# State-space mixer: decays, convolution and product moved off GpSimd; h formed anew with the norm's row; banks emptied by ScalarE

## The chip, the cores and the metric

One core of one Trainium2 chip. The metric is the device time of one execution, in microseconds (us). Names used below: PE is TensorE (PEld its weight loads), DVE is VectorE, ACT is ScalarE, POOL is GpSimd, SP the queue that issues most transfers.

## The reference, cut to what matters

Twelve units follow one another on 256 tokens of width 1024: a first block (two mixers, a feed-forward, a mixture of experts) and a second block. The unit of this case is the state-space mixer of the second block:

```
proj = h @ w_in                                    # h = rmsnorm(x) * gain; 1024 -> 8256
z, xbc, dt_raw = split(proj)
xbc = silu(conv5(xbc, conv_w) + conv_b)            # centred depthwise, 5 taps
xs, b_f, c_f, b_b, c_b = split(xbc)                # 32 heads of 64; 8 groups, state 128
dt = softplus(dt_raw + dt_bias);  cum = cumsum(dt * a)
scores = (c @ b^T) * exp(where(lower, cum_q - cum_k, -inf)) * dt_k
y = scores @ xs  + the same run backwards  + xs * d_skip
y = rmsnorm(y * silu(z)) @ w_out
```

With 256 tokens and chunks of 128 each direction has three 128x128 blocks per head: two on the diagonal, which are masked, and one beside it, which is not.

## The kernel before, in words

The tokens lie along the free axis, the channels on the partitions. Every weight of 128x2048 numbers is loaded by SP into a `wraw` tile (three in flight) and split into a high and a low part, in two halves: ScalarE writes `whi` (L211), VectorE writes `wlo` as the difference (L212). A product is three matmuls (`mm3`, L269): high by high, high by low, low by high. `proj` (L518) takes one weight, makes 2x8x3 = 48 matmuls into a PSUM bank `pj` (three of them) and hands the bank to a function that empties it.

The mixer's method is `ssd` (L1920). Its operands `hh`, `hl` are the split of x times the gain, made while the unit before ends; the norm's factor 1/rms per token (`st["r"]`, a row copied to all partitions at L484) is not in them, and each bank is multiplied by that row when it is emptied. First come the step sizes: `ssd_dt` (L1854) turns a 64x256 bank into dt and its running sum `cum` by some 25 short VectorE instructions, writes `cum` to DRAM as `cumd` (L1881), and transposes three tables of log-factors into `stok`. Then eight groups g of four heads follow; each has four projections:

- `x`, `f`, `b` (`conv`, L1929): VectorE empties the bank into a padded tile `cz*` (L1931), ScalarE makes the first tap with the bias (L1936), and four more taps for two 128-channel halves follow, each a multiply-add of 128x256 on VectorE (`stt`, L287); for the second half of `x` POOL does them, as a product (L1942) and a sum (L1943). ScalarE applies Silu (L1947).
- `z` (`gate`, L1950): VectorE empties the bank times the row into `sz` (L1952), ScalarE applies Silu (L1953).

`ssd_decay` (L1896) makes the decays E of a group, for each direction a tile of 4 heads x 3 blocks x 128 (128x1536): SP reads the rows of `cumd` to all partitions into `crow` (L1903, two transfers, one buffer), POOL subtracts the per-partition table (L1911), adds a mask of -1e30 (L1912) and forms the block beside the diagonal (L1915), five instructions of 128x512 per direction; ScalarE takes the exponential (L1917). It is called at the end of group g; `scan(g)` (L1956) runs in group g+1 behind the `f` projection: transposes of xs to `xd` (L1966), the c-by-b matmuls into a bank, and a VectorE product of E with that bank (L1975, 128x1536). `scan_out(g)` (L1978) comes behind the `z` projection of group g+1: sixteen matmuls of E with xd, the skip term on VectorE (L1989), the product with `sz` on POOL (L1990), ScalarE's high half `yh` (L1994), VectorE's low half `yl` (L1995), and ScalarE's squares that POOL adds up (`sq_add`, L417 to L420). After group 7 the output projection runs as a `Down` (L569), whose matmuls need the four `acc` banks.

Each engine works its instructions off in a fixed order. That order is made when the kernel is built: a scheduler goes by the program's order, in which `first()` (L264) and `high_priority(...)` pull instructions forward, and by its estimate of when inputs are ready.

Of the kernel before, what the change touches and what calls it, by code (L numbers as in the profile page):

```python
# [10 lines left out]
F32 = mybir.dt.float32  # L11
# [8 lines left out]
T = 256  # L20
# [7 lines left out]
NEG = -1e30  # L28

# [217 lines left out]
class Kernel:  # L247
# [1587 lines left out]
    def ssd_consts(self, pool):  # L1835
# [3 lines left out]
        for m, op in zip(S["mask"], (OP.is_lt, OP.is_gt)):  # L1839
            nc.vector.tensor_scalar(m, self.jp, 0.0, NEG, op0=op, op1=OP.mult)  # L1840
# [13 lines left out]
    def ssd_dt(self, pool, b, r):  # L1854
# [31 lines left out]
        for o, c, l in ((0, 0, 127), (32, 1, 128)):  # L1886
            rs, cs = slice(o, o + 32), slice(c * 128, (c + 1) * 128)
            self.stt(off[rs], dt[rs, cs], cum[rs, l:l + 1], cum[rs, cs], OP.add, OP.subtract)
        v.tensor_sub(p, cum, dt)
        b = self.bank("ms")  # L1890
        for i, src in enumerate((p[:, 0:128], p[:, 128:256], off)):
            self.tr(b[:, 64 * i:64 * (i + 1)], src)
# [3 lines left out]
    def ssd_decay(self, pool, g):  # L1896


        nc, S = self.nc, self.S
        cr = pool.tile([128, 2, 4, T], F32, name="crow", bufs=1)  # L1900
        src = S["dram"].rearrange("(r h) t -> r h t", r=2)[:, 4 * g:4 * g + 4, :]
        for r in range(2):
            nc.sync.dma_start(cr[:, r], src[r][None].to_broadcast([128, 4, T]))  # L1903
        out = []
        for r in range(2):
            E = pool.tile([128, 4, 3, 128], F32, name="E", bufs=3)
            hs = slice(4 * g, 4 * g + 4)
            for c in range(2):
                d = E[:, :, 2 * c, :]
                cc = S["tok"][:, c, r, hs][:, :, None].to_broadcast([128, 4, 128])  # L1910
                nc.gpsimd.tensor_sub(d, cr[:, r, :, c * 128:(c + 1) * 128], cc)  # L1911
                nc.gpsimd.tensor_add(d, d, S["mask"][r][:, None, :].to_broadcast([128, 4, 128]))  # L1912
            oc = S["tok"][:, 2, r, hs][:, :, None].to_broadcast([128, 4, 128])
            t = slice(128, 256) if r == 0 else slice(0, 128)
            nc.gpsimd.tensor_add(E[:, :, 1, :], cr[:, r, :, t], oc)  # L1915
            out.append(E)
            nc.scalar.activation(E, E, AF.Exp)  # L1917
        return out

    def ssd(self, pool, tail):  # L1920
# [8 lines left out]
        def conv(n, g, b):  # L1929
            z = S["cz"][n, g % 2 if n == "x" else 0]  # L1930
            v.tensor_mul(z[:, :, 2:T + 2], v2(b), st["r"][:, None, :].to_broadcast([128, 2, T]))  # L1931
# [5 lines left out]
            for k in range(1, 5):  # L1937
                for j in range(2):
                    w = cw[:, 48 * k + tl[j]:48 * k + tl[j] + 1]
                    if n == "x" and j:  # L1940
                        t = pool.tile([128, T], F32, name="cvt", bufs=1)
                        nc.gpsimd.tensor_mul(t, z[:, j, k:k + T], w.to_broadcast([128, T]))  # L1942
# [573 lines left out]
```

## Time and profile before

| | us |
|---|---|
| runs | 2808.49, 2814.82, 2814.09 (median 2814.09) |
| the profiled execution | 2806.44 |
| its span, first to last instruction | 2804.6 |
| PE busy | 2622.2 (93%) |
| DVE busy | 2178.5 (78%) |
| ACT busy | 1582.7 (56%) |
| POOL busy | 564.0 (20%) |

The profiled execution lies 7.65 us under the median of the runs, and 1.8 us of its time lie outside the span. The shares are means over twelve units with different limits, so the mixer is read by its own stretch: the norm's row is ready at 1693 us, the gates of the eight groups are emptied between 1722.7 and 1974.5 us, and the last scan ends at about 1990 us.

### The profile page before, as it was taken

What the parts mean: (1) busy time and instruction counts of PE and PEld (TensorE: products, weight loads), DVE (VectorE), ACT (ScalarE), POOL (GpSimd) and SP (SyncE); (2) the same over time, 40 slices, a digit from 0 to 9 for tenths busy, and PEclk for the clock granted to TensorE, in tenths of its full rate; (3) what the DMA queues carried; (4) which work ended last, traced back from release to release, by engine and by line L of the source; (5) the groups of instructions that cost most, each with busy time, mean ns of one, the idle gap of its engine ahead of it and who ended that gap; (6) DMA issues with size and microseconds to landing.
All of it is one profiled execution on the core that took longest, in us unless ns stands there. A gap on an engine that the chain in (4) does not pass through costs nothing. (4 is left out here: it accounts for less than half of the span.)

```text
span 2804.6 us, 50551 instructions
## 1 busy us (share of the span) xinstructions
PE 2622.2 (93%) x20739; PEld 2446.0 (87%) x20739; DVE 2178.5 (78%) x3100; ACT 1582.7 (56%) x2222; POOL 564.0 (20%) x490
## 2 busy tenths in 40 slices
PE   8999968989999999999998998887899999989999
PEld 6789967789999999999778997777799999979998
DVE  6989986869998999988876568999665675665666
ACT  5343336657777777777663445766444454465444
POOL 2413982310000000000000005776110010240000
PEclk9999988999999999999998999999999999999999
DMA  7476764256999999999763554434445555552553
GB/s 276 167 270 248 279 210 150 91 214 258 349 338 355 339 353 365 342 325 372 250 213 140 197 178 152 151 139 147 151 166 196 186 175 193 195 188 72 182 194 121
DMA packets 109203, 623.07 MB, mean 222 GB/s; under 512 B 10049, under 2 KB 10065, under 8 KB 56353
## 3 DMA queue, kind: packets, MB, share of 16 engines
q1 hardware_dynamic: 107664, 612.05, 61.2%
q0 software_dynamic: 1296, 7.68, 0.7%
q8 instruction: 165, 2.70, 0.4%
q14 instruction: 78, 0.63, 0.1%
HBM read 616.49 MB, written 3.21 MB: 221 GB/s over the span
## 5 line engine op out<-in xcount | busy, mean ns | idle before, releaser
L212 DVE TENSOR_TENSOR wlo<-wraw,whi 128x1024 fp32r<-128x1024 f32 (+1 forms) x1046 | 1284.3, 1265 | 250.1 <-ACT whi L211 247.3
L211 ACT ACTIVATE whi<-wraw 128x1024 fp32r<-128x1024 f32 (+1 forms) x1046 | 1046.5, 1050 | 668.6 <-issue 353.8
L269 PE MATMUL pj<-hh,whi 128*128 128x256 f32 (+1 forms) x2672 | 757.8, 284 | 54.0 <-DVE czb L1931 38.5
L269 PE MATMUL pj<-hh,wlo 128*128 128x256 f32 (+1 forms) x2672 | 754.3, 282 | 4.1 <-DVE wlo L212 4.0
L269 PE MATMUL pj<-hl,whi 128*128 128x256 f32 (+1 forms) x2672 | 754.2, 282 | 1.2 <-DVE hl L287 1.2
L269 PEld LDWEIGHTS pj<-hh,whi 128*128 128x128 f32 (+1 forms) x2672 | 514.9, 193 | 58.9 <-issue 29.3
L269 PEld LDWEIGHTS pj<-hh,wlo 128*128 128x128 f32 (+1 forms) x2672 | 514.4, 193 | 7.9 <-DVE wlo L212 6.8
L269 PEld LDWEIGHTS pj<-hl,whi 128*128 128x128 f32 (+1 forms) x2672 | 514.8, 193 | 3.0 <-DVE hl L287 2.3
L269 PE MATMUL pj<-whi,hg 128*128 128x256 f32 x2112 | 382.2, 279 | 0.0
L269 PEld LDWEIGHTS pj<-whi,hg 128*128 128x128 f32 x2112 | 325.6, 188 | 11.2 <-issue 8.7
L269 PE MATMUL pj<-wlo,hg 128*128 128x256 f32 x1056 | 294.0, 278 | 0.0
L269 PE MATMUL acc<-mh,whi 128*128 128x256 f32 x880 | 245.5, 279 | 13.9 <-ACT whi L211 13.9
L269 PE MATMUL acc<-mh,wlo 128*128 128x256 f32 x880 | 245.8, 279 | 7.0 <-DVE wlo L212 7.0
L269 PE MATMUL acc<-ml,whi 128*128 128x256 f32 x880 | 245.7, 279 | 1.6 <-DVE ml L284 1.6
L269 PEld LDWEIGHTS pj<-wlo,hg 128*128 128x128 f32 x1056 | 198.6, 188 | 3.7 <-issue 2.1
L269 PEld LDWEIGHTS acc<-mh,whi 128*128 128x128 f32 x880 | 167.2, 190 | 14.1 <-ACT whi L211 14.1
L441 POOL TENSOR_TENSOR rc<-var,mhalf 128x2 f32<-128x2 f32 x2 | 1.4, 705 | 878.4 <-DVE var L1803 877.1
L417 POOL TENSOR_TENSOR ss<-sq 128x256 f32<-128x256 f32 x11 | 11.9, 1083 | 825.1 <-ACT sq L410 592.2
L269 PEld LDWEIGHTS acc<-mh,wlo 128*128 128x128 f32 x880 | 167.1, 190 | 8.1 <-DVE wlo L212 8.1
L269 PEld LDWEIGHTS acc<-ml,whi 128*128 128x128 f32 x880 | 167.1, 190 | 2.2 <-DVE ml L284 2.2
L269 PE MATMUL acc<-whi,mml 128*128 128x512 f32 x352 | 139.1, 399 | 0.7 <-DVE mml L284 0.7
L269 PE MATMUL acc<-wlo,mmh 128*128 128x512 f32 x352 | 139.6, 397 | 0.0
(721 smaller groups left out, 4424.6 us busy)
## 6 DMA issues: line engine op xcount, KB each, us to landing
wraw<-in_o_exp_down_dram SPq DMA_DIRECT2D x88, 1024.0 KB, 5.8
wraw<-in_ffn_w_gu_dram SPq DMA_DIRECT2D x88, 1024.0 KB, 5.0
wraw<-in_o_exp_gate_dram SPq DMA_DIRECT2D x87, 1024.0 KB, 5.9
wraw<-in_o_exp_up_dram SPq DMA_DIRECT2D x87, 1024.0 KB, 6.0
wraw<-in_ffn_w_down_dram SPq DMA_DIRECT2D x44, 1024.0 KB, 5.1
wraw<-in_ssd_cols_dram SPq DMA_DIRECT2D x32, 1024.0 KB, 4.9
wraw<-in_e_mod_ffn_w_t_dram SPq DMA_DIRECT2D x12, 1024.0 KB, 5.0
wraw<-in_o_mod_mix_w_t_dram SPq DMA_DIRECT2D x12, 1024.0 KB, 5.0
```

Source lines behind the costliest of these rows:

```text
L211: nc.scalar.activation(hi[:, cs], t[:, cs], AF.Copy)
L212: nc.vector.tensor_sub(lo[:, cs], t[:, cs], f32(hi[:, cs]))
L269: self.nc.tensor.matmul(out, lhsT, rhs, start=start, stop=stop, skip_group_check=True)
L417: nc.gpsimd.tensor_add(ss[0], sq[:, 0, :], sq[:, 1, :])
L441: nc.gpsimd.tensor_tensor(r, v, self.mhalf.to_broadcast([128, n]), op=OP.pow)
```

## The change

- E is loaded directly: SP reads the rows of `cumd` into the E tiles themselves (four transfers per group in place of two, 1.5 times the bytes written; four E buffers instead of three; `crow` is gone). VectorE subtracts the whole table at once (128x1536), clamps the two diagonal blocks from above at 88.722 (128x1024, every third block left out), ScalarE takes the exponential as before. `ssd_decay(g)` is called behind the `x` projection of group g instead of at its end.
- The mask becomes a table of 0 and 1 and moves from the exponent to the c-by-b bank: VectorE writes the two masked blocks (128x256) and ScalarE copies the third (128x128) into a new SBUF tile `scb`; the product with E then has both inputs in SBUF.
- The taps of the second half of `x` become VectorE multiply-adds; the product with `sz` goes to VectorE.
- h is formed anew once the row 1/rms is there: eight VectorE instructions of 128x256 (x times gain times row) and four splits of 128x512 (ScalarE copy, VectorE difference), with raised priority. From then on the banks need no factor: ScalarE empties them (`conv` by a copy, `gate` by Silu straight from the bank). The banks of dt and of the first `x`, which were multiplied before, keep the factor on VectorE.

```diff
--- before.py
+++ after.py
@@ -26,6 +26,8 @@
 MID = 3
 EPS = 1e-6
 NEG = -1e30
+
+LOGMAX = 88.722
 
 SPLIT_ORDER = {"s": -30, "f1_0": -100, "e": -200, "f2_0": 50}
 
@@ -1836,8 +1838,8 @@
         nc = self.nc
         S = self.S = {}
         S["mask"] = [pool.tile([128, 128], F32, name=f"smask{i}") for i in range(2)]
-        for m, op in zip(S["mask"], (OP.is_lt, OP.is_gt)):
-            nc.vector.tensor_scalar(m, self.jp, 0.0, NEG, op0=op, op1=OP.mult)
+        for m, op in zip(S["mask"], (OP.is_ge, OP.is_le)):
+            nc.vector.tensor_scalar(m, self.jp, 0.0, None, op0=op)
         go = S["go"] = pool.tile([64, T], F32, name="sgo")
         nc.gpsimd.memset(go, 1.0)
         nc.gpsimd.memset(go.rearrange("p (c i) -> p c i", i=128)[:, :, 0:1], 0.0)
@@ -1885,10 +1887,10 @@
         off = s2[:, 0:128]
         for o, c, l in ((0, 0, 127), (32, 1, 128)):
             rs, cs = slice(o, o + 32), slice(c * 128, (c + 1) * 128)
-            self.stt(off[rs], dt[rs, cs], cum[rs, l:l + 1], cum[rs, cs], OP.add, OP.subtract)
+            self.stt(off[rs], cum[rs, cs], cum[rs, l:l + 1], dt[rs, cs], OP.subtract, OP.subtract)
         v.tensor_sub(p, cum, dt)
         b = self.bank("ms")
-        for i, src in enumerate((p[:, 0:128], p[:, 128:256], off)):
+        for i, src in enumerate((p[:, 0:128], off, p[:, 128:256])):
             self.tr(b[:, 64 * i:64 * (i + 1)], src)
         tok = S["tok"] = pool.tile([128, 3, 2, 32], F32, name="stok")
         v.tensor_copy(tok, b[:, :192].rearrange("p (i r h) -> p i r h", i=3, r=2))
@@ -1896,28 +1898,23 @@
     def ssd_decay(self, pool, g):
 
 
+
         nc, S = self.nc, self.S
-        cr = pool.tile([128, 2, 4, T], F32, name="crow", bufs=1)
         src = S["dram"].rearrange("(r h) t -> r h t", r=2)[:, 4 * g:4 * g + 4, :]
-        for r in range(2):
-            nc.sync.dma_start(cr[:, r], src[r][None].to_broadcast([128, 4, T]))
         out = []
         for r in range(2):
-            E = pool.tile([128, 4, 3, 128], F32, name="E", bufs=3)
-            hs = slice(4 * g, 4 * g + 4)
-            for c in range(2):
-                d = E[:, :, 2 * c, :]
-                cc = S["tok"][:, c, r, hs][:, :, None].to_broadcast([128, 4, 128])
-                nc.gpsimd.tensor_sub(d, cr[:, r, :, c * 128:(c + 1) * 128], cc)
-                nc.gpsimd.tensor_add(d, d, S["mask"][r][:, None, :].to_broadcast([128, 4, 128]))
-            oc = S["tok"][:, 2, r, hs][:, :, None].to_broadcast([128, 4, 128])
-            t = slice(128, 256) if r == 0 else slice(0, 128)
-            nc.gpsimd.tensor_add(E[:, :, 1, :], cr[:, r, :, t], oc)
+            E = pool.tile([128, 4, 3, 128], F32, name="E", bufs=4)
+            for i, n, t in ((0, 2, 0), (2, 1, 128)) if r == 0 else ((0, 1, 0), (1, 2, 0)):
+                nc.sync.dma_start(E[:, :, i:i + n, :].rearrange("p h i t -> p h (i t)"), src[r][None, :, t:t + n * 128].to_broadcast([128, 4, n * 128]))
             out.append(E)
+        for r, E in enumerate(out):
+            cc = S["tok"][:, :, r, 4 * g:4 * g + 4].rearrange("p i h -> p h i")
+            nc.vector.tensor_sub(E, E, cc[:, :, :, None].to_broadcast([128, 4, 3, 128]))
+            nc.vector.tensor_scalar(E[:, :, 0::2, :], E[:, :, 0::2, :], LOGMAX, None, op0=OP.min)
             nc.scalar.activation(E, E, AF.Exp)
         return out
 
-    def ssd(self, pool, tail):
+    def ssd(self, pool, gain, tail):
         nc, S = self.nc, self.S
         v = nc.vector
         v2 = lambda b: b.rearrange("p (a t) -> p a t", a=2)
@@ -1928,7 +1925,10 @@
 
         def conv(n, g, b):
             z = S["cz"][n, g % 2 if n == "x" else 0]
-            v.tensor_mul(z[:, :, 2:T + 2], v2(b), st["r"][:, None, :].to_broadcast([128, 2, T]))
+            if (n, g) == ("x", 0):
+                v.tensor_mul(z[:, :, 2:T + 2], v2(b), st["r"][:, None, :].to_broadcast([128, 2, T]))
+            else:
+                nc.scalar.activation(z[:, :, 2:T + 2], v2(b), AF.Copy)
             c = pool.tile([128, 2, T], F32, name="cv" + n, bufs=2)
             cw, cb = self.v["conv_w"], self.v["conv_b"]
             tl = conv_t[n](g)
@@ -1937,20 +1937,14 @@
             for k in range(1, 5):
                 for j in range(2):
                     w = cw[:, 48 * k + tl[j]:48 * k + tl[j] + 1]
-                    if n == "x" and j:
-                        t = pool.tile([128, T], F32, name="cvt", bufs=1)
-                        nc.gpsimd.tensor_mul(t, z[:, j, k:k + T], w.to_broadcast([128, T]))
-                        nc.gpsimd.tensor_add(c[:, j], c[:, j], t)
-                    else:
-                        self.stt(c[:, j, :], z[:, j, k:k + T], w, c[:, j, :], OP.mult, OP.add)
+                    self.stt(c[:, j, :], z[:, j, k:k + T], w, c[:, j, :], OP.mult, OP.add)
             with self.tc.high_priority(offset=-100) if n == "x" else nullcontext():
                 nc.scalar.activation(c, c, AF.Silu)
             D_[n, g] = c
 
         def gate(g, b):
             z = pool.tile([128, 2, T], F32, name="sz", bufs=2)
-            v.tensor_mul(z, v2(b), st["r"][:, None, :].to_broadcast([128, 2, T]))
-            nc.scalar.activation(z, z, AF.Silu)
+            nc.scalar.activation(z, v2(b), AF.Silu)
             D_["z", g] = z
 
         def scan(g, tag="acc"):
@@ -1969,10 +1963,13 @@
                 c0, c1 = slice(0, 128), slice(128, 256)
                 for i, (s, t) in enumerate(((c0, c0), (c0, c1) if r == 0 else (c1, c0), (c1, c1))):
                     self.mm(b[:, i * 128:(i + 1) * 128], bc[:, 0, s], bc[:, 1, t], i == 0, i == 2)
-                cb = b[:, None, 0:384].to_broadcast([128, 4, 384])
+                cb = pool.tile([128, 3, 128], F32, name="scb", bufs=2)
+                b = b[:, 0:384].rearrange("p (i t) -> p i t", i=3)
                 e = E[r].rearrange("p h i t -> p h (i t)")
                 with self.tc.high_priority(offset=100):
-                    v.tensor_mul(e, e, cb)
+                    v.tensor_mul(cb[:, 0::2], b[:, 0::2], S["mask"][r][:, None, :].to_broadcast([128, 2, 128]))
+                    nc.scalar.activation(cb[:, 1], b[:, 1], AF.Copy)
+                    v.tensor_mul(e, e, cb.rearrange("p i t -> p (i t)")[:, None, :].to_broadcast([128, 4, 384]))
             D_["s", g] = E, xs, xd, sz
 
         def scan_out(g, tag="acc"):
@@ -1987,7 +1984,7 @@
             for j in range(2):
                 d = 2 * g + j
                 self.stt(xs[:, j, :], xs[:, j, :], self.v["ssd_d"][:, d:d + 1], yb[:, j * T:(j + 1) * T], OP.mult, OP.add)
-            nc.gpsimd.tensor_mul(sz, sz, xs)
+            v.tensor_mul(sz, sz, xs)
             gn = self.v["ssd_norm"]
             for j in range(2):
                 d = 2 * g + j
@@ -2005,6 +2002,14 @@
                 self.mm3(b1[:, j * T:(j + 1) * T], (w1[0][:, k, js], w1[1][:, k, js]), self.h(k), j == 0 and k == 0, k == KD - 1)
         st["r"] = self.norm_end()[1]
         self.W.done(("ssd", "dt"), ("ssd", "x", 0))
+
+        with self.first():
+            for p in range(4):
+                t = self.act.tile([128, 2, T], F32, name="sq", bufs=2)
+                for j in range(2):
+                    k = 2 * p + j
+                    self.stt(t[:, j, :], self.x[:, k, :], gain[:, k:k + 1], st["r"], OP.mult, OP.mult)
+                self.split(self.hh[:, 2 * p:2 * p + 2, :], self.hl[:, 2 * p:2 * p + 2, :], t)
         self.ssd_dt(pool, b0, st["r"])
         conv("x", 0, b1)
         for g in range(8):
@@ -2013,10 +2018,11 @@
                     self.proj([("ssd", n, g)], lambda i, b: conv(n, g, b))
                 if n == "f" and g:
                     scan(g - 1)
+                if n == "x":
+                    D_["E", g] = self.ssd_decay(pool, g)
             self.proj([("ssd", "z", g)], lambda i, b: gate(g, b))
             if g:
                 scan_out(g - 1)
-            D_["E", g] = self.ssd_decay(pool, g)
         row = {}
 
         def t2(p, acc):
@@ -2466,7 +2472,7 @@
             elif u == "ssd":
                 with tc.tile_pool(name="ssd", bufs=1) as sp:
                     self.ssd_consts(sp)
-                    self.ssd(sp, after(u))
+                    self.ssd(sp, v[gains["ssd"]][:, 0:8], after(u))
             elif u == "na":
                 with tc.tile_pool(name="nac", bufs=1) as nac:
                     with tc.tile_pool(name="nat", bufs=1) as nat:
```

## Rows read from the trace of the kernel before

**Rows 1.** The page's 40 equal slices of the span (70.1 us each), busy tenths.

```profile
DVE  6989986869998999988876568999665675665666
...
POOL 2413982310000000000000005776110010240000
```

**Rows 2.** Busy time by stretch: length, PE, PEld, DVE, ACT, POOL, granted clock, DMA share, GB/s.

```profile
1722.70:1974.50 251.80, 192.82 (x1578) 183.13 (x1578) 235.26 (x254) 157.68 (x188) 182.05 (x153) 0.90 0.41 142
...
1693.00:1990.00 297.00, 233.47 (x1893) 221.65 (x1893) 277.22 (x326) 185.34 (x223) 195.13 (x166) 0.90 0.41 144
...
1990.00:2010.00 20.00, 20.00 (x172) 20.00 (x171) 10.40 (x10) 8.46 (x11) 0.30 (x1) 1.00 0.46 161
```

**Rows 3.** Chain of waits from 1722.7 to 1974.5 us: its shares by engine and line.

```profile
by line: DVE wlo L212 27.0%; DVE cvf L287 20.6%; DVE cvx L287 9.6%; DVE E L1975 7.6%; DMA crow<-cumd 5.2%; issue 5.1%; DVE cvb L287 3.7%; POOL E L1911 3.3%; POOL sz L1990 3.3%; DVE yl L287 3.0%; POOL E L1912 2.8%; ACT yh L1994 1.2%; DVE czb
```

**Rows 4.** DVE groups, 1693 to 1990 us: count, busy us, mean ns, idle before, releaser.

```profile
L212 DVE TENSOR_TENSOR wlo<-wraw,whi 128x1024 fp32r<-128x1024 f32 x62 | 93.9, 1544 | 0.0
...
L287 DVE SCALAR_TENSOR_TENSOR cvf<-czf,vecs,cvf 128x256 f32<-128x256 f32 x64 | 60.9, 1002 | 0.0
...
L287 DVE SCALAR_TENSOR_TENSOR cvx<-czx,vecs,cvx 128x256 f32<-128x256 f32 x32 | 26.8, 837 | 0.2
...
L287 DVE SCALAR_TENSOR_TENSOR cvb<-czb,vecs,cvb 128x256 f32<-128x256 f32 x64 | 26.4, 478 | 0.2
...
L1975 DVE TENSOR_TENSOR E<-E,acc 128x1536 f32<-128x1536 f32 x14 | 23.9, 1744 | 6.2 <-ACT E L1917 6.2
...
L287 DVE SCALAR_TENSOR_TENSOR yl<-sz,vecs,yh 128x256 fp32r<-128x256 f32 x14 | 12.7, 948 | 10.0 <-ACT yh L1994 10.0
...
L1952 DVE TENSOR_TENSOR sz<-pj,rstd 128x512 f32<-128x512 f32 x8 | 5.4, 679 | 0.0
```

**Rows 5.** Two tiles, DVE lines: count: ns min/median/max, first and last start.

```profile
L287 DVE SCALAR_TENSOR_TENSOR cvf<-czf,vecs,cvf x64: 467/1255/1515, 1707.8 to 1971.2; 128x256 f32<-128x256 f32 x64
...
L1975 DVE TENSOR_TENSOR E<-E,acc x14: 1740/1742/1755, 1733.7 to 1959.5; 128x1536 f32<-128x1536 f32 x14
```

**Rows 6.** DVE groups from 1400 to 1680 us, the expert stage and the feed-forward after it.

```profile
L212 DVE TENSOR_TENSOR wlo<-wraw,whi 128x1024 fp32r<-128x1024 f32 x100 | 120.7, 1222 | 42.1 <-ACT whi L211 42.0
...
L284 DVE TENSOR_TENSOR ml<-gu,mh 128x512 fp32r<-128x512 f32 x11 | 7.6, 692 | 0.7 <-ACT mh L283 0.7
```

**Rows 7.** POOL groups from 1693 to 1990 us.

```profile
L1912 POOL TENSOR_TENSOR E<-E,smask 128x512 f32<-128x512 f32 x32 | 50.4, 1587 | 0.0
...
L420 POOL TENSOR_TENSOR ssb<-ssb,sq 128x256 f32<-128x256 f32 x6 | 6.7, 1110 | 0.3
...
L419 POOL TENSOR_TENSOR sq<-sq 128x256 f32<-128x256 f32 x6 | 5.4, 899 | 2.1 <-ACT sq L410 2.1
```

**Rows 8.** DVE groups of one instruction each, 1700 to 2000 us, two kinds.

```profile
L1869 DVE TENSOR_TENSOR dtq<-dts 64x256 f32<-64x256 f32 x1 | 0.4, 407 | 0.0
...
L1870 DVE TENSOR_SCALAR dtp<-dtq 64x256 f32<-64x256 f32 x1 | 0.3, 274 | 0.0
```

**Rows 9.** ACT groups from 1693 to 1990 us.

```profile
L1917 ACT ACT_TABLE_LOAD x15 | 19.2, 1283 | 0.3
...
L1966 ACT ACTIVATE xd<-acc 128x512 f32<-128x512 f32 x7 | 4.0, 576 | 0.0
```

**Rows 10.** Timeline of DVE, 1690 to 1742 us: start, length, instruction.

```profile
1693.13 0.42 DVE L484 COPY rstd<-ms 128x256 f32<-128x256 f32 x1 [0.61 <-PE ms L269]
...
1704.07 0.67 DVE L1931 TENSOR_TENSOR czf<-pj,rstd 128x512 f32<-128x512 f32 x1
...
1713.58 0.67 DVE L1931 TENSOR_TENSOR czb<-pj,rstd 128x512 f32<-128x512 f32 x1
```

**Rows 11.** Waits from 1693 to 1990 us: total us, times, longest.

```profile
PE pj L269 <- DVE czb L1931: 48.8, 7, 10.3
...
POOL E L1911 <- DMA crow<-cumd: 21.8, 2, 11.8
```

**Rows 12.** Tile crow: DMA issue to landing.

```profile
DMA to landing us min/median/max: 3.6/6.6/8.1
```

## The prediction

> **What bounds the kernel now.** I read the page's slices first, to find where POOL works at all: only from slice 24 on, where the mixer is, is it busy half the time or more, beside some early slices [rows 1]. Then the table by stretch. Between the first and the last emptied gate lie 251.8 us for seven group periods, 36.0 us each. VectorE is busy 235.3 of them (93%), PE 192.8, POOL 182.1, ScalarE 157.7; the granted clock of PE is 0.90, while right after the mixer, where PE never pauses, it is 1.00 and 172 matmuls take 20 us, 0.116 us each [rows 2]. Third, the chain of waits of that stretch: it runs nearly all along VectorE's lines, the splits `wlo` (27%) and the taps (20.6% for `cvf` alone), with a few short pieces on POOL and on the transfer of `crow` [rows 3]. PE, the engine that bounds most of the kernel, waits here for VectorE to empty banks: 48.8 us in 7 waits [rows 11]. So a group costs what VectorE needs for it.
>
> The fourth view, VectorE's groups, shows why it needs so much [rows 4]. The tap is one instruction of 128x256 whatever the tile, yet it takes 478 ns on `cvb`, 837 on `cvx` and 1002 on `cvf`; and on `cvf` alone it goes from 467 to 1515 ns [rows 5]. A split takes 1544 ns here and 1222 in the expert stage, where POOL has almost nothing to do [rows 6]. The product of E with a PSUM bank, by contrast, took 1740 to 1755 ns in all 14 cases [rows 5]. I read this as POOL and VectorE slowing each other where VectorE reads SBUF alone: POOL is busy 195 us of the stage [rows 2].
>
> **The change part by part**, summed over the stage from 1693 us (the norm's row) to 1990 us (the last scan), 297 us, of which VectorE is busy 277.2 and idle 19.8 [rows 2]. Its backlog is the path, so its terms count in full.
>
> *POOL's work goes, relief.* What POOL keeps are the sums of squares, 12.1 us [rows 7]. VectorE's own instructions should fall to their undisturbed price: 62 splits from 93.9 to 62 x 1.207 = 74.8 (120.7/100, [rows 6]), -19.1; 64 `cvf` taps from 60.9 to the 26.4 that 64 `cvb` taps took, -34.5; 32 `cvx` taps from 26.8 to 32 x 0.4125 = 13.2, -13.6; 14 `yl` from 12.7 to 5.8, -6.9 [rows 4]. Together -74.1; I leave 12.1/195 of it, 4.6, for the work that POOL keeps: **-69.5**.
>
> *POOL's work comes to VectorE.* The subtraction: 16 of 128x1536, by the product of the same size 23.9/14 = 1.707 [rows 4]: +27.3. The clamp: 16 of 128x1024 with a constant, which the trace does not have. Of two instructions of 64x256, one with two tensors took 407 ns and one with a constant 274 [rows 8], so a constant form seems to run at twice the rate, and I price the clamp like a two-tensor instruction of half its size, 0.692 [rows 6]: +11.1; the upper bound is a split of 128x1024, 1.207, +19.3. The mask on the bank: 16 of 128x256, as a tap, 0.4125: +6.6. Taps: 32 x 0.4125 = +13.2. The product with `sz`: 8 x 0.692 = +5.5. h anew: 8 x 0.4125 and 4 x 0.692 = +6.1. The new product of E with `scb` stays at its size, 0. Together **+69.8**.
>
> *Emptying goes to ScalarE.* 23 conv banks and 8 gates at 5.4/8 = 0.675 [rows 4]: **-20.9**.
>
> VectorE's busy time: 277.2 - 69.5 + 69.8 - 20.9 = 256.6, -20.6.
>
> *Its idle time.* Of 19.8 us, 10.0 are waits of `yl` for ScalarE's `yh`, which stands behind POOL's product with `sz`, and 6.2 waits of the product for E, which stands behind POOL's work on it [rows 4]. Both causes go; late next will be `scb`, whose third block ScalarE copies before the product may start, and E's transfer. The bounds are none left (-19.8) and as much as before (0); I take the middle, **-9**, since one new wait replaces each old one at a shorter producer. Sum: **-30**.
>
> *Costed at nothing.* ScalarE gets 23 copies of a bank at 0.576 (as `xd`, [rows 9]), 16 copies of a quarter of that, at most 0.576 each, and 4 splits: 13.2 + 9.2 + 2.8 = 25 us on 185.3 busy, 210 of some 267: covered, as long as it does not stand behind VectorE. The table loads, 1.283 us each [rows 9], go on alternating between Silu and the exponential, and I count none more. PE has 233.5 us busy in the stage, at a clock of 0.90 [rows 2], and gets no matmul more, so it stays below 267. SP: four transfers in place of two per group in SP's queue, with 1.5 times the bytes; weight loads stand behind them, but weights are requested three ahead, and the transfers of `crow` already waited in that queue for POOL. E's buffers are freed by the scan two groups back, which ends on PE just before the `x` projection. The exponential is needed a group later, and landing took 3.6 to 8.1 us [rows 12]; no wait is counted. In the first group, E needs `cumd`, which h's 6.1 us on VectorE push back, while POOL's turn over E (50.4 us in 32 mask additions alone, 1.6 each, [rows 7]) falls out of that path.
>
> *PE's hold at the start.* Before, PE goes from the first `x` straight into `f` on the unscaled h, and the row comes at 1693.1 + 0.4 [rows 10]. Now `f` waits: first pair two of 0.41, a copy of 0.58, a difference of 0.69, about 1695.6; last pair 6.1 us after the row, about 1699.7. `f` then ends near 1702 instead of some ten us earlier (48 x 0.116 = 5.6 us). But its bank was emptied only at 1704.07 and the next at 1713.6 [rows 10], because VectorE was behind: the cover is VectorE's backlog, and the hold costs nothing. Without the cover it is 10 us.
>
> One rule speaks against the change. The product of E had a PSUM input and was steady; from now on both its inputs are in SBUF. The Trainium skill (GPSIMD Engine Reference, section 1, Specifications) says that GpSimd's SBUF interface is shared with VectorE and that the contention arises with two SBUF inputs or a two-port mode; by it the product loses its immunity, and were each of the 12.1 us of POOL that is left to stretch it by a half, the sum would be -24 instead of -30. The trace agrees as to which instructions suffer (1740 to 1755 with PSUM, 467 to 1515 without).
>
> **The rivals.**
> *Smaller gain (0.13).* PE's hold is not covered (+10), or the clamp runs at full rate (+8.3) with idle time as before (+9): -20 to -13, 2794 to 2801. For it: three engines at four fifths and more, each in a fixed order. Against: VectorE's backlog is what the chain shows.
>
> *E's transfer stalls VectorE: slower (0.08).* The subtraction now stands in VectorE's fixed order with splits and taps behind it; if its transfer has not landed, all wait, and PE behind them. POOL did wait for `crow`, 21.8 us in two waits [rows 11]. A whole median landing of 6.6 us [rows 12] in each group is +53, net +23, 2837. It decides from 30/8 = 3.8 us per group on. Against: the `x` projection (5.6 us on PE) and its emptying come between, and the scheduler may put the subtraction later.
>
> *The relief isn't there: slower (0.03).* If the taps are slow for another reason than POOL (where the tiles lie), the stage gets +69.8 - 20.9 - 9 = +40, 2854. Against: the same `cvf` tap at 467 ns, too.
>
> *The gain is lost elsewhere (0.08).* ScalarE, in order, hands banks over late because a copy stands behind exponentials and splits. With 30 us more of ScalarE waits on the path nothing is left: 2814.
>
> **How the numbers follow.** The profiled execution took 2806.4; -30 gives 2776. The runs' median is 7.7 above it, so on the median of 2814.1 the forecast is **2784** (chance 0.68). Its own range: idle time all gone is -40, and runs have come 5.6 below the median: 2768, and some us less if splits in a row run faster still; the dear clamp with idle as before is -13, 2801. Range 2765 to 2806, which leaves out the slower cases. A change of 0.3%, 8.4 us, is about what a measurement of this kernel tells from none. Faster by more than that: forecast and smaller gain, less what the latter's tail gives back, 0.80; same 0.09; slower 0.11.
>
> **What would show it.** Right: `cvf` taps near 0.48 and splits near 1.2 us in the mixer; gates some 32 us apart; VectorE about 257 us busy between the row and the last scan; the product of E still near 1.75; the clamp near 0.7; the waits of PE for a bank's emptying by VectorE gone. Wrong: VectorE idle for an E transfer in every group; taps still at 0.8 to 1.0; gates 35 us apart or more; ScalarE named as releaser of PE in long waits.

## Result and the profile after

| | before | changed |
|---|---|---|
| median of the four runs, us | 2811.29 (2806.66 to 2814.82) | 2771.52 (2767.01 to 2779.78) |
| profiled execution, us | 2806.44 | 2767.01 |
| its span, us | 2804.6 | 2765.2 |
| row 1/rms to the end of the last scan, us | 294.8 | 261.9 |
| from there to the first output product `ot`, us | 40.4 | 34.3 |

The changed kernel takes 0.9863 of the time before (95% interval 0.9831 to 0.9894). The forecast was -30 us, the medians differ by 39.8 and the spans by 39.4. Of these, 32.9 fall between the norm's row and the last scan, 6.1 between the last scan and the first output. Before the norm's row, where the two kernels do the same work but for the mask table, the changed execution was 5.0 us ahead (its row came at 1688.2 in place of 1693.1), and behind the first output it lost 4.5 us. No run here explains these two, and that they cancel is chance: in the other runs below the row came anywhere from 1686.9 to 1700.3 us, and what follows the first output took 778 to 794 us.

The page's slices of the changed kernel, VectorE and POOL (to set against [rows 1]):

```profile
DVE  6989986868998999989876568999665765665666
...
POOL 2413992320000000000000001011100100331000
```

POOL has all but gone out of the mixer (slices 24 to 28); what it does in the other units is as before. The table by stretch: seven group periods, row to last scan, last scan to first output; columns as in [rows 2]:

```profile
1714.60:1926.40 211.80, 195.72 (x1649) 186.52 (x1648) 203.84 (x302) 155.11 (x215) 21.27 (x11) 0.95 0.58 193
1688.10:1950.10 262.00, 238.38 (x1973) 226.59 (x1972) 250.96 (x390) 183.38 (x251) 22.80 (x14) 0.94 0.53 178
1950.10:1984.40 34.30, 33.75 (x288) 33.55 (x287) 21.00 (x29) 15.15 (x17) 1.23 (x2) 1.00 0.50 185
```

A period is 211.8/7 = 30.3 us instead of 36.0, VectorE is busy 96% of it, and the granted clock rose from 0.90 to 0.95. From row to last scan VectorE is busy 250.96 us and idle 11.0; the prediction had 256.6 and about 11. The chain of waits over the seven periods (against [rows 3]):

```profile
by line: PE pj L271 24.1%; DVE wlo L214 13.5%; DVE E L1972 10.7%; DVE E L1912 10.3%; DVE cvx L289 9.0%; ACT whi L213 4.6%; DMA wraw<-in_ssd_cols_dram 4.1%; DMA E<-cumd 3.5%; DVE cvb L289 3.4%; DVE E L1913 2.9%; DVE cvf L289 2.8%; DVE yl L28
```

The splits fell from 27% to 13.5%, `cvf` from 20.6% to 2.8%. E's product (L1972) rose from 7.6% to 10.7%, its subtraction (L1912) is new on the chain, and PE's projections have become its longest piece (24.1%): two engines now share the path. VectorE's groups from 1690 to 1955 us, which takes in the same 14 `yl` as [rows 4]:

```profile
L214 DVE TENSOR_TENSOR wlo<-wraw,whi 128x1024 fp32r<-128x1024 f32 x64 | 77.2, 1236 | 0.2 <-ACT whi L213 0.2
L1972 DVE TENSOR_TENSOR E<-E,scb 128x1536 f32<-128x1536 f32 x16 | 30.7, 1920 | 0.0
L1912 DVE TENSOR_TENSOR E<-E,stok 128x1536 f32<-128x1536 f32 x16 | 27.4, 1749 | 1.4 <-DMA E<-cumd 1.3
L289 DVE SCALAR_TENSOR_TENSOR cvx<-czx,vecs,cvx 128x256 f32<-128x256 f32 x64 | 26.4, 473 | 0.0
L289 DVE SCALAR_TENSOR_TENSOR cvb<-czb,vecs,cvb 128x256 f32<-128x256 f32 x64 | 26.4, 475 | 0.0
L289 DVE SCALAR_TENSOR_TENSOR cvf<-czf,vecs,cvf 128x256 f32<-128x256 f32 x64 | 26.3, 475 | 0.0
L1913 DVE TENSOR_SCALAR E<-E 128x1024 f32<-128x1024 f32 x16 | 10.4, 682 | 0.0
L289 DVE SCALAR_TENSOR_TENSOR yl<-sz,vecs,yh 128x256 fp32r<-128x256 f32 x14 | 6.2, 482 | 4.0 <-ACT yh L1991 4.0
...
L1970 DVE TENSOR_TENSOR scb<-acc,smask 128x256 f32<-128x256 f32 x14 | 5.9, 420 | 2.5 <-PE acc L271 2.5
L1987 DVE TENSOR_TENSOR sz<-sz,cvx 128x512 f32<-128x512 f32 x8 | 5.5, 685 | 0.1
```

All three kinds of tap now take 473 to 475 ns, a split 1236, `yl` 482. The clamp takes 682 ns for 1024 elements. The waits from row to last scan (against [rows 11]):

```profile
PE pj L271 <- DVE wlo L214: 14.3, 6, 3.7
...
DVE yl L289 <- ACT yh L1991: 4.0, 4, 1.6
...
PE pj L271 <- ACT sz L1947: 1.1, 3, 0.4
...
DVE E L1912 <- DMA E<-cumd: 1.3, 1, 1.3
```

PE no longer waits for VectorE to empty a bank; it waits 14.3 us for splits, which VectorE also makes. E's transfer held VectorE once, for 1.3 us.

### The profile page after: what moved, and what is told of

Its sections match the earlier page's. It is cut to its first block, busy times and chain, and to the rows that moved or that the text cites. A ratio compares the mean times of both kernels' runs of the same rounds, so it can differ in the third digit from the quotient of the medians.

```text
span 2765.2 us, 50492 instructions
## 1 busy us (share of the span) xinstructions
PE 2617.9 (95%) x20739; PEld 2441.9 (88%) x20739; DVE 2156.8 (78%) x3169; ACT 1579.3 (57%) x2251; POOL 392.0 (14%) x338
## 5 line engine op out<-in xcount | busy, mean ns | idle before, releaser
L214 DVE TENSOR_TENSOR wlo<-wraw,whi 128x1024 fp32r<-128x1024 f32 (+1 forms) x1046 | 1264.5, 1246 | 240.1 <-ACT whi L213 237.4
L271 PE MATMUL acc<-whi,mmh 128*128 128x512 f32 x352 | 137.3, 407 | 0.0
```

The costliest lines, as they stand in the source:

```text
L214: nc.vector.tensor_sub(lo[:, cs], t[:, cs], f32(hi[:, cs]))
L271: self.nc.tensor.matmul(out, lhsT, rhs, start=start, stop=stop, skip_group_check=True)
```

## The experiments

"Stage" is the stretch from the norm's row to the end of the last scan, in the profiled execution. The changed kernel's is 261.9 us, and 264.5 in a second execution of it (below), so differences under some 3 us say nothing. Several 95% intervals below overlap that of the changed kernel (0.9831 to 0.9894); there the stage decides, and not the median.

**POOL busy with work that nobody waits for (e1_idle_pool_work).** This separates the two readings of the gain: VectorE slowed by POOL's work as such, or by waits for POOL's results.

```diff
             self.sq_add(g, sz, ssy, last=7)
+            if g < 6:
+                dm = pool.tile([128, 2, T], F32, name="dm", bufs=1)
+                one = ssy[0][:, None, :].to_broadcast([128, 2, T])
+                for _ in range(16):
+                    nc.gpsimd.tensor_add(dm, one, one)
```

> The changed kernel with POOL kept busy again by work that no other engine waits for: behind the sums of squares of groups 0 to 5, 16 additions of 128x512 into a tile that nobody reads (some 20 to 25 us per group). Shared-reading theory (POOL and VectorE slow each other where VectorE reads two SBUF tensors, and VectorE's backlog is the path): the taps rise from 0.475 to 0.8 to 1.0 us while POOL runs; 195 us of POOL cost 74 us of VectorE before, so some 130 us cost about 50: stage from the norm's row to the last scan 262 to about 310 us, total about 2820. Order theory (what counted was that others waited for POOL, not that it worked): taps stay at 0.475, total stays at about 2772.

Measured: 2853.48 us, 1.0131 of before (1.0087 to 1.0175). The stage by engine (columns as in [rows 2]) and three groups of VectorE:

```profile
1695.50:2029.40 333.90, 248.24 (x1971) 233.33 (x1971) 328.10 (x390) 183.57 (x251) 165.28 (x108) 0.85 0.42 139
```

```profile
L289 DVE SCALAR_TENSOR_TENSOR cvx<-czx,vecs,cvx 128x256 f32<-128x256 f32 x64 | 64.1, 1060 | 0.0
L1912 DVE TENSOR_TENSOR E<-E,stok 128x1536 f32<-128x1536 f32 x16 | 37.6, 2382 | 1.1 <-DMA E<-cumd 1.1
...
L1913 DVE TENSOR_SCALAR E<-E 128x1024 f32<-128x1024 f32 x16 | 20.5, 1315 | 0.0
```

The stage is 333.9 us, +72. VectorE's busy time is 328.1, +77.1, for 142.5 us more of POOL (165.3 - 22.8): 0.54 us per us, and half as much again as the 50 us expected. The timeline shows it without any mean: eight taps of `cvb` while POOL rests and eight of `cvx` while it adds, first VectorE, then POOL:

```profile
1844.37 3.25 DVE L289 SCALAR_TENSOR_TENSOR cvb<-czb,vecs,cvb 128x256 f32<-128x256 f32 x8
...
1859.04 9.51 DVE L289 SCALAR_TENSOR_TENSOR cvx<-czx,vecs,cvx 128x256 f32<-128x256 f32 x8
1868.47 5.10 DVE L1912 TENSOR_TENSOR E<-E,stok 128x1536 f32<-128x1536 f32 x2
1873.50 2.97 DVE L1913 TENSOR_SCALAR E<-E 128x1024 f32<-128x1024 f32 x2
```

```profile
1829.05 10.46 POOL L1998 TENSOR_TENSOR dm<-ssb 128x512 f32<-128x512 f32 x6
...
1857.58 23.74 POOL L1998 TENSOR_TENSOR dm<-ssb 128x512 f32<-128x512 f32 x15
```

3.25 us against 9.51 us for the same eight instructions. The order theory falls: nobody waited for this work, and it cost more than the whole gain.

Read instruction by instruction, the two engines take turns: inside each of the sixteen additions from 1857.6 to 1882.5 us one VectorE instruction begins, and it pays about the same, whatever its size: a tap takes 1.26 us for 0.47, a split of 128x1024 2.06 for 1.22, a subtraction of 128x1536 2.59 for 1.75. So the price can be counted by POOL's instructions: 77.1 us for 96 additions of 128x512, 0.80 us each.

**One input, and none.** The same, with 24 copies (`tensor_copy(dm, one)`) or 32 memsets (behind an addition of 8 columns that ties them to the group) in place of the 16 additions.

> As e1_idle_pool_work, but POOL's idle work is 24 copies of 128x512 per group, one input in place of two. If the slowing comes from POOL's reading as such, VectorE's busy time grows by about half of POOL's added time, as there (0.54); if it takes two inputs on POOL's side, by less than a fifth of it.

> As e1_idle_pool_work, but POOL's idle work is 32 memsets of 128x512 per group: it writes and reads nothing. If the slowing is a matter of reading, VectorE's taps stay at 0.475 and its busy time at 251; if writing counts too, both grow.

Measured, one run each: copies 2831.24 us, stage 308.9, VectorE busy 304.1 (+53 for 140 us more of POOL, 0.38 us per us, or 0.37 us for each of the 144 copies); memsets 2772.4 us, stage 263.8, VectorE busy 251.5 for 115 us more of POOL. Eight `cvx` taps under copies, and POOL at that time:

```profile
1811.45 6.06 DVE L289 SCALAR_TENSOR_TENSOR cvx<-czx,vecs,cvx 128x256 f32<-128x256 f32 x8
```

```profile
1809.98 20.29 POOL L1998 COPY dm<-ssb 128x512 f32<-128x512 f32 x19
```

and under memsets:

```profile
1798.30 3.24 DVE L289 SCALAR_TENSOR_TENSOR cvx<-czx,vecs,cvx 128x256 f32<-128x256 f32 x8
```

```profile
1798.50 19.73 POOL L1998 MEMSET dm<- 128x512 f32 x32
```

6.06 us under copies, 3.24 under memsets. Here POOL's reading slows VectorE, more with two inputs than with one; its writing does not.

**The decays back on POOL.** `ssd_decay`, its call at the group's end, the mask in the exponent and the product straight from the bank as in the kernel before; the rest as changed. In short:

```diff
...
-                cb = pool.tile([128, 3, 128], F32, name="scb", bufs=2)
...
-                    v.tensor_mul(e, e, cb.rearrange("p i t -> p (i t)")[:, None, :].to_broadcast([128, 4, 384]))
+                    v.tensor_mul(e, e, b[:, None, 0:384].to_broadcast([128, 4, 384]))
...
-                if n == "x":
-                    D_["E", g] = self.ssd_decay(pool, g)
...
+            D_["E", g] = self.ssd_decay(pool, g)
```

> The changed kernel with the decays back on POOL (crow, five instructions per direction, mask in the exponent, product straight from the bank, called at the group's end); taps, the product with sz, h and the emptying stay as changed. Shared-reading theory: VectorE loses 44 us of work (subtraction 27, clamp 10, mask 7) and gets 114/195 of the old slowing back, 43: its busy time stays at about 251; with E late again by some waits (+6) the total is 2772 to 2785. Order theory: POOL's lateness was the cost, so most of the gain goes, 2795 to 2810.

Measured: 2798.89 us, 0.9947 of before (0.9926 to 0.9968), 27 over the changed kernel. VectorE's groups and the stage:

```profile
L214 DVE TENSOR_TENSOR wlo<-wraw,whi 128x1024 fp32r<-128x1024 f32 x62 | 87.8, 1449 | 0.0
L289 DVE SCALAR_TENSOR_TENSOR cvf<-czf,vecs,cvf 128x256 f32<-128x256 f32 x64 | 56.5, 945 | 0.0
L289 DVE SCALAR_TENSOR_TENSOR cvb<-czb,vecs,cvb 128x256 f32<-128x256 f32 x64 | 32.0, 569 | 0.0
```

```profile
1690.90:1966.40 275.50, 236.73 (x1923) 226.92 (x1923) 269.49 (x342) 196.97 (x248) 137.36 (x92) 0.90 0.43 153
```

The total lies where the order theory had it, but not for its reason: VectorE is idle 6.0 us of 275.5, less than in the changed kernel, and busy 269.5, 18.5 more. It lost 44.5 us of work and 3.3 of the product, and was slowed by 66 us, 0.58 per us of POOL's 114.6 instead of the 0.38 that I had from the kernel before. So the price of a microsecond of POOL is not fixed. For each of the 80 instructions of 128x512 that came back to POOL it is 0.83 us, near the 0.80 of the idle additions. That it was less in the kernel before, because VectorE read PSUM banks for more of the time, is argued and not tested. Of the 27 us, 13.6 are in the stage and another 5.8 before the first output; in the profiled executions the other 7.6 lie before the norm's row (2.7) and behind the first output (4.9), where the work is the same.

**The banks emptied by VectorE.** No new h, all banks times the row on VectorE; POOL's part stays moved.

```diff
...
-            if (n, g) == ("x", 0):
-                v.tensor_mul(z[:, :, 2:T + 2], v2(b), st["r"][:, None, :].to_broadcast([128, 2, T]))
-            else:
-                nc.scalar.activation(z[:, :, 2:T + 2], v2(b), AF.Copy)
+            v.tensor_mul(z[:, :, 2:T + 2], v2(b), st["r"][:, None, :].to_broadcast([128, 2, T]))
...
-            nc.scalar.activation(z, v2(b), AF.Silu)
+            v.tensor_mul(z, v2(b), st["r"][:, None, :].to_broadcast([128, 2, T]))
+            nc.scalar.activation(z, z, AF.Silu)
...
```

> The changed kernel with the emptying of all banks back on VectorE, times the norm's row, and no new h. Backlog theory: VectorE gets 20.9 us and loses 6.1, +15 us: about 2786, stage 277 us. Rival (PE's waits for a bank were the cost, 48.8 us before, and are gone because ScalarE empties): +30 to +45, 2800 to 2815.

Measured: 2780.29 us, 0.9875 (0.9832 to 0.9918), 9 over the changed kernel. The stage:

```profile
1700.30:1973.80 273.50, 239.94 (x1951) 225.64 (x1950) 266.91 (x412) 171.93 (x226) 12.81 (x14) 0.95 0.50 171
```

VectorE is busy 266.9 us, +16.0 (expected +15), the stage is 273.5, +11.6. The 9 us of the medians alone would not be clear of noise; the stage is. The 48.8 us for which PE waited for banks before were thus a sign of VectorE's backlog, and not a cost of that size of their own.

**The taps of `x` back on POOL.**

```diff
-                    self.stt(c[:, j, :], z[:, j, k:k + T], w, c[:, j, :], OP.mult, OP.add)
+                    if n == "x" and j:
+                        t = pool.tile([128, T], F32, name="cvt", bufs=1)
+                        nc.gpsimd.tensor_mul(t, z[:, j, k:k + T], w.to_broadcast([128, T]))
+                        nc.gpsimd.tensor_add(c[:, j], c[:, j], t)
+                    else:
+                        self.stt(c[:, j, :], z[:, j, k:k + T], w, c[:, j, :], OP.mult, OP.add)
```

> The changed kernel with the taps of the second half of x back on POOL (32 products and 32 sums of 128x256). Shared-reading theory: VectorE loses 13.2 us of taps and gets 57/195 of the old slowing, 22: +9 us, about 2780; the cvx taps that stay rise above 0.7 us. Order theory: VectorE does 13 us less and nothing else changes, 2758 to 2772.

Measured: 2787.24 us, 0.991 (0.9879 to 0.9941), 16 over the changed kernel. Two groups of VectorE and one of POOL:

```profile
L1912 DVE TENSOR_TENSOR E<-E,stok 128x1536 f32<-128x1536 f32 x16 | 34.7, 2167 | 1.2 <-DMA E<-cumd 1.2
...
L289 DVE SCALAR_TENSOR_TENSOR cvx<-czx,vecs,cvx 128x256 f32<-128x256 f32 x32 | 24.7, 772 | 0.0
```

```profile
L1943 POOL TENSOR_TENSOR cvx<-cvx,cvt 128x256 f32<-128x256 f32 x32 | 49.3, 1542 | 3.6 <-ACT cvx L1936 1.5 <-DVE yl L289 0.3
```

VectorE does 32 taps less and is busy 12.6 us more (263.5, in a stage of 277.6): the subtraction of E rose from 1749 to 2167 ns, the taps of `x` that stayed on it from 473 to 772. POOL is slowed too: its sum takes 1542 ns, 923 in the kernel before. 12.6 of the 16 us are VectorE's: 25.8 of slowing for 80.2 us more of POOL (103.0 - 22.8), less the 13.2 of the taps. By POOL's instructions it is 0.40 us for each of the 64, which are half the size of the idle additions.

**The emptying alone (e5_emptying_alone).** The kernel before with the new h (the same lines as in the change, left out here) and the emptying by ScalarE; decays, taps and product stay on POOL.

```diff
...
-            v.tensor_mul(z[:, :, 2:T + 2], v2(b), st["r"][:, None, :].to_broadcast([128, 2, T]))
+            if (n, g) == ("x", 0):
+                v.tensor_mul(z[:, :, 2:T + 2], v2(b), st["r"][:, None, :].to_broadcast([128, 2, T]))
+            else:
+                nc.scalar.activation(z[:, :, 2:T + 2], v2(b), AF.Copy)
...
-            v.tensor_mul(z, v2(b), st["r"][:, None, :].to_broadcast([128, 2, T]))
-            nc.scalar.activation(z, z, AF.Silu)
+            nc.scalar.activation(z, v2(b), AF.Silu)
...
```

> The kernel before with one part of the change alone: h formed anew and all banks but two emptied by ScalarE; POOL keeps decays, taps and product. Backlog theory: VectorE 20.9 - 6.1 = 15 us shorter, stage 295 to about 280, total 0.995 of before (2798). Rival (PE's 48.8 us of waits for banks were the cost): 0.983 to 0.988, nearly the whole gain.

Measured: 2833.27 us, 1.0065 (1.0044 to 1.0087): slower than before, against both theories. The stage and two waits:

```profile
1690.70:1997.40 306.70, 239.21 (x1898) 224.19 (x1898) 256.39 (x305) 179.81 (x236) 190.38 (x165) 0.89 0.39 138
```

```profile
ACT E L1917 <- POOL E L1915: 41.0, 8, 7.0
...
DVE cvx L287 <- ACT cvx L1939: 26.8, 6, 5.6
```

VectorE's work did fall, by 20 us to 256.4, but it is now idle for 50.3 us of 306.7. ScalarE's exponential waits 41 us for POOL's E (10.5 in the kernel before), and the copies of banks and first taps stand behind it in ScalarE's order; VectorE's taps wait 26.8 us for them. The same part that is worth some 9 us with the decays off POOL costs 19 with them on it.

**The same, with the exponentials later.** To take ScalarE's queue out of it, the exponentials of a group get a bias of zero made from the next group's f bank, so that they stand behind its emptying.

```diff
             out.append(E)
-            nc.scalar.activation(E, E, AF.Exp)
...
             E = D_.pop(("E", g))
+            zb = pool.tile([128, 32], F32, name="zb", bufs=1)[:, 0:1]
+            nc.scalar.activation(zb, S["cz"]["f", 0][:, 0, 2:3], AF.Copy, scale=0.0)
+            for e in E:
+                nc.scalar.activation(e, e, AF.Exp, bias=zb)
```

> The kernel with the emptying alone (e5_emptying_alone), but the exponentials of a group stand behind the emptying of the next group's f bank in ScalarE's order (their bias is a zero made from that bank's copy). Queue theory (in e5_emptying_alone the emptying stood behind exponentials that waited 41 us for POOL): ScalarE's wait for POOL's E falls below 10 us, and the total from 2833 to 2795 to 2812, under the kernel before. Rival (ScalarE's emptying is dear by itself): 2820 to 2835.

Measured: 2855.32 us, 1.0144 (1.0114 to 1.0175), a miss. The waits:

```profile
PE acc L269 <- DVE E L1980: 81.5, 14, 11.7
...
ACT cvx L1949 <- POOL cvx L1945: 59.2, 7, 9.8
POOL E L1911 <- PE acc L269: 56.4, 6, 9.5
...
ACT E L1962 <- POOL E L1915: 10.2, 1, 10.2
```

The exponential's wait for POOL did fall, from 41.0 to 10.2 us, about as expected; but E now reaches its product late, PE's scan waits for that, POOL waits for PE to free an E buffer (56.4 us), and the tap sums on POOL, behind E in POOL's order, come late for ScalarE (59.2 us). So the waits of the emptying alone are shown, but how much of its 19 us is the queue on ScalarE stays open: moving the exponentials moved the waits into a ring of POOL, ScalarE, VectorE and PE.

**The changed kernel again, and PE's hold filled.** The first is the measure for the next two; in the second, the `f` projection of group 0 runs on the unscaled h while the norm is finished.

```diff
...
-            if (n, g) == ("x", 0):
+            if (n, g) in (("x", 0), ("f", 0)):
...
+        f0 = {}
+        self.proj([("ssd", "f", 0)], lambda i, b: f0.update(b=b))
         with self.first():
...
-                if (n, g) != ("x", 0):
+                if (n, g) == ("f", 0):
+                    conv(n, g, f0["b"])
+                elif (n, g) != ("x", 0):
                     self.proj([("ssd", n, g)], lambda i, b: conv(n, g, b))
```

> The changed kernel once more, beside the runs below, as their measure. Every theory: stage (norm's row to last scan) 262 us, total 0.983 to 0.989 of before.

> The changed kernel with the f projection of group 0 made on the unscaled h while the norm is finished, its bank emptied by VectorE with the row; PE's hold before the new h is filled with 48 matmuls. Cover theory (VectorE's backlog hides PE's hold): total within 2 us of the changed kernel, at most 0.7 us slower for VectorE. Rival (the hold is on the path): 5 to 6 us faster.

Measured: 2770.87 us for the changed kernel (0.9863, 0.9831 to 0.9894), 2772.65 with the hold filled (0.9853, 0.9823 to 0.9882). The intervals are too wide to rule out the rival's 5 to 6 us; the traces do better. VectorE has no gap of 0.1 us in the first 26 us behind the row, with the hold or without it. And PE's wait was only moved: with `f` made ahead, PE stands from 0.3 to 8.8 us behind the row (in the changed kernel it starts at 2.0), and the emptying of `b`'s bank begins 19.1 us behind the row, 19.2 in the changed kernel (20.5 before). PE's hold was hidden, as the prediction had it.

**The decays at the group's end.**

```diff
-                if n == "x":
-                    D_["E", g] = self.ssd_decay(pool, g)
...
+            D_["E", g] = self.ssd_decay(pool, g)
```

> The changed kernel with the decays of group g made at the group's end, as before, instead of behind its x projection. Backlog theory: the seven periods stay at 30 us, as VectorE's work is the same; only the last group's E is exposed (transfer 6, subtractions, clamps and exponentials some 8): stage 262 to 268 to 276, total +6 to +14. Rival (E has slack everywhere): within 3 us of the changed kernel.

Measured: 2768.87 us, 0.9831 (0.9795 to 0.9866), within 3 us of the changed kernel. The stage:

```profile
1694.10:1953.80 259.70, 240.68 (x2044) 230.19 (x2044) 255.85 (x395) 188.23 (x256) 14.54 (x14) 0.96 0.53 179
```

259.7 us: the last group's E is not exposed. The earlier call buys nothing; the gain is in who does the work. It may even cost: from the row to the first output this version takes 284.8 us, the changed kernel 296.3 and in its second execution 298.9, because more of the output projection is done before the last scan (25.0 us from there to the first output in place of 34.3). Of that only 2 to 3 us arrive in the median, since what follows took 792 us here and 781 and 783 there, which no run explains.

**The clamp on ScalarE.** A step further along the same line: VectorE is the path and ScalarE has room. The bound is 20 instead of 88.722; it touches only entries that the mask then makes zero, unless a step size exceeds exp(20).

```diff
+        top = S["top"] = pool.tile([128, 32], F32, name="stop")[:, 0:1]
+        nc.gpsimd.memset(top, 20.0)
...
-            nc.vector.tensor_scalar(E[:, :, 0::2, :], E[:, :, 0::2, :], LOGMAX, None, op0=OP.min)
-            nc.scalar.activation(E, E, AF.Exp)
+            nc.scalar.activation(E, E, AF.Relu, scale=-1.0, bias=S["top"])
+            nc.scalar.activation(E, E, AF.Exp, scale=-1.0, bias=S["top"])
```

> The changed kernel with the clamp moved from VectorE to ScalarE: Relu(20 - x) over all of E, then exp(20 - that), instead of VectorE's minimum. Backlog theory: VectorE loses its 10.4 us of clamps, ScalarE gets some 25 on 183: stage 262 to about 252, total 8 to 10 us under the changed kernel. Rival (ScalarE or PE is by now the path as much as VectorE): stage unchanged or a few us longer.

Measured: 2762.52 us, 0.9808 of before (0.9781 to 0.9836); the changed kernel beside it took 2770.87. The stage:

```profile
1690.80:1940.00 249.20, 230.90 (x1972) 219.24 (x1972) 241.95 (x374) 221.55 (x279) 16.97 (x12) 0.97 0.55 187
```

VectorE 241.95 us busy (-9), ScalarE 221.55 (+38), stage 249.2 us. It is 8.4 us under the changed kernel by the medians, as VectorE's work says, though the two intervals overlap a little. By the medians it is the fastest version here.

## Why the prediction was right

*What bounds the kernel.* Right. The run with POOL's idle work shows both halves: POOL's work alone slows VectorE, and VectorE's added 77 us come out as 72 us of stage and 82 of total (the other 10 lie outside the stage).

*The relief.* Right to the term: splits 93.9 to 74.9 (74.8 said), `cvf` 60.9 to 26.3 (26.4), `cvx` 26.4 for 64 taps (twice 13.2), `yl` 12.7 to 6.2 (5.8).

*The work that came.* Subtraction 27.4 (27.3 said), clamp 10.4 (11.1), mask 6.7 (6.6), product with `sz` 5.5 (5.5). A constant operand does run at nearly twice the rate (682 ns for 1024 elements, a split 1236), and the dear bound of 19.3 falls. Luck had a part in that: the two rows it was read from, 407 and 274 ns, differ by a factor of 1.5 only.

*The product of E.* Costed at nothing, and mis-sized: 30.7 us against 23.9 + 3.5 = 27.4 before, +3.3. The timeline shows where, VectorE first, then POOL:

```profile
1789.80 1.75 DVE L1972 TENSOR_TENSOR E<-E,scb 128x1536 f32<-128x1536 f32 x1
...
1793.16 2.29 DVE L1972 TENSOR_TENSOR E<-E,scb 128x1536 f32<-128x1536 f32 x1
```

```profile
1789.96 2.20 POOL L421 TENSOR_TENSOR sq<-sq 128x256 f32<-128x256 f32 x1 [27.36 <-ACT sq L412]
1792.23 1.60 POOL L422 TENSOR_TENSOR ssb<-ssb,sq 128x256 f32<-128x256 f32 x1
```

The first of these two products began just ahead of a POOL addition and kept its 1.75 us; the addition took 2.20, where the last group's, with no such product beside it, takes 0.73. The second began while the next POOL addition was still on, and took 2.29. So it is in the whole stage: six products overlap a POOL addition that began with them or behind them, by 1.6 us or more, and stay at 1.75; five begin inside one and take 2.29. The one that comes second waits. That is the exposure which the Trainium skill's rule (GPSIMD Engine Reference, section 1, Specifications) gives to an instruction with two SBUF inputs; the trace agrees, with five products slowed by 0.54 us each, within the 0 to 6 us that the prediction allowed. The 4.6 us that I left for POOL's remaining work happen to cover it, though I had put them on the splits and taps. And that remaining work took POOL 22.8 us instead of 12.1, because its additions wait for VectorE in turn.

*Sum of busy time.* -25.4 measured (276.35 from 1693.1 to 1987.9 us before, 250.96 now) against -20.6. The named terms come to about -22. Two of the 14 `yl` and one of the 8 products with `sz` now fall behind the last scan, some 1.6 us, and the short instructions of the step sizes lost some slowing too (`dts` by `dte` went from 824 to 409 ns); I had counted neither.

*Idle time.* From 18.4 to 11.0 us, -7.4 against -9.

*ScalarE.* Forecast at 210 us busy, measured 183.4. One term was put at nothing that was not: the table loads fell from 33 to 19 in the stage, 18 us. ScalarE did not bound the stage, so this cost the forecast nothing.

*What was missed.* The step "summed over the stage to the last scan" ended too soon: the end of the mixer is the output projection. One row of the kernel before and one of the changed kernel, matmuls of `yh` with the high halves until the last scan ends:

```profile
L269 PE MATMUL acc<-yh,whi 128*128 128x256 f32 x16 | 5.6, 352 | 0.0
```

```profile
L271 PE MATMUL acc<-yh,whi 128*128 128x256 f32 x33 | 9.9, 308 | 0.0
```

16 against 33: 17 more, and with the two other matmuls that go with each some 50, which at 0.116 us [rows 2] are 5.9 us. That is nearly all of the 6.1 by which the time from the last scan to the first output fell. PE had reached the output projection while VectorE was still at the last group. This term is 6 of the 9 to 10 us by which the gain exceeded the forecast of 30; the rest is in the stage (-32.9).

*The rivals.* E's transfer did not stall VectorE (1.3 us once). PE's hold was covered (VectorE did not stand still in the first 26 us behind the row, and the run that fills the hold gains nothing). The relief was there. ScalarE as the one that hands banks over late did not happen in the whole change, but waits of that kind are what the emptying alone shows: the parts depend on each other. Undone one by one, in the changed kernel, they cost 27 (decays), 16 (taps) and 9 us (emptying) by the medians. From the row to the first output that is 19, 15 and 9, together 43 against 39 for the whole, so these three alone would not show a dependence; the 19 us that the emptying costs by itself do.

## What to carry to other kernels

When the mean of an elementwise instruction differs between like tiles (0.48 against 1.0 us here), suspect a neighbour: set the timelines of VectorE and POOL side by side before counting engines' shares. In this kernel, work put on a "free" POOL that reads SBUF was paid for on VectorE at a third to more than a half of its time, so work moved off POOL made VectorE's total shorter although VectorE does it. And try the parts alone: one that helps in company may cost where its engine stands in line behind the work that was not moved.

## What the hardware showed that I had not expected

- POOL's memsets, 115 us more of POOL in the stage, left VectorE's taps at 472 to 478 ns; copies took eight taps from 3.25 to 6.06 us, additions to 9.51. It is POOL's reading that counted here.
- The clamp, one SBUF input and a constant, is slowed as well: 682 to 1315 ns under POOL's additions.
- A microsecond of POOL cost VectorE 0.32 (taps), 0.38 (the whole kernel before; copies), 0.54 (additions) or 0.58 us (decays), so one ratio does not carry over from one mix to another. Per POOL instruction it was steadier: 0.80 and 0.83 us for 128x512 with two inputs, 0.40 for 128x256, 0.37 for a copy of 128x512.
- Where POOL's sums of squares met E's product, the one that started second waited, and that fell on either engine: a POOL addition that takes 0.73 us by itself took 2.2 beside a product of 1.75 us that had begun before it, and a product that had begun inside an addition took 2.29.
